# Delta rule of a hybrid block: two heads per sweep, and four heads per sweep with its copies in two portions

## Chip, cores and metric

The kernel runs on one core of one Trainium2 chip. The metric is the device time of one execution in microseconds (us), the median of the executions taken; the profile's span goes from the first to the last instruction of one execution.

## What is computed

One layer of a bidirectional encoder block on 256 tokens of 2048 channels: an input projection whose columns feed an mLSTM branch, a gated delta rule branch with 16 heads of 128, and merge gates, then an output projection and a SwiGLU. All of it is float32. The part that the change touches is the delta rule, forward and backward in time, head by head:

```python
    qkv = jax.nn.silu(centred_depthwise_conv(b_qkv, gdn_conv_w))
    ...
    a_mat = jnp.eye(CHUNK, dtype=jnp.float32) + (
        betac[..., :, None] * jnp.einsum('nbhid,nbhjd->nbhij', kc, kc) * decay_strict)
    t_mat = lax.linalg.triangular_solve(
        a_mat, jnp.broadcast_to(jnp.eye(CHUNK, dtype=jnp.float32), a_mat.shape),
        left_side=True, lower=True, unit_diagonal=True)
    ...
    o_b = bidirectional(gated_delta_chunkwise, (q_b, k_b, v_b), (beta[0], log_decay[0]), (beta[1], log_decay[1]))
    o_b = rms_norm(o_b.transpose(0, 2, 1, 3), gdn_norm_w.reshape(B_HEADS, B_DV)).reshape(bsz, t, B_V)
```

## The kernel before

**Projections.** A weight tile of 1 MB arrives by DMA on SyncE's queue and is used in two halves. Of each half ScalarE makes a high part `wh` (line 181 in `fjob`, 213 in `tjob`), VectorE the rest `wl` (lines 183 and 215), and TensorE multiplies high by high, high by low and low by high. `wh` and `wl` have three buffers each, so ScalarE can make a new `wh` only when TensorE is through with the half three before. `fjob` makes the b jobs (the delta rule's q, k and v: three jobs of two halves per head, 24 matmuls of 128x256 a half) and the a jobs; `tjob` makes everything else (ma and mb for the merge gates, z, v, o), 12 matmuls of 128x512 a half. The jobs that nothing waits for at once are *fills*: `fill(n)` issues n halves of the next one in the list.

**Order.** Every engine works through its own queue in the order in which the program issues. What shall not stand ahead of the next `wh` is appended to a list `behind`; `settle()`, called right after each `wh` copy, issues what is in it. `pump()`, called once per half, issues another piece of the adaptive modulation now and then: one multiplication of a 128x2048 tile on VectorE (line 125, `ada`) with its DMA on SyncE; it is held back in the first three steps of a sweep (`held`).

**A head of the delta rule.** After each of its b jobs comes the convolution (`gdn_conv`: copy into a padded tile `pad`, line 346; ScalarE's first tap `cv`, line 349; four taps on VectorE, line 351; SiLU to `kq` or `vf`, line 354). Then comes the head's first phase (`gdn_phase1`, in two pieces): decays (line 653), `kqh` and `kql` (660, 661), squares `sqkq` (663), on TensorE `vps` (666: vf turned; 668: sums of squares), `nn` and `vv` (678, 688), on TensorE `ks` (699 to 701), on VectorE the masked products `mi`, `mb`, `gg`, `at` (706 to 716), their 32x32 diagonal blocks to memory by GpSimd's queue, and on ScalarE the off-diagonal corners `cc` (738, 741).

**A group of four heads.** `gdn_invert` inverts all 32x32 blocks of a group on VectorE, beside fills. Then `gdn_phase2(g, p)` makes two heads in each of two sweeps, p = 0 and 1, in nine steps with small matmuls (128x32 to 128x128) that each need what ScalarE or VectorE made of the step before: p1 (line 822) and its masked copy `pt` (823); p2 (831), transposed on VectorE and copied into `X` (834 to 838); p3 (844), `pt` (845), copies into `UL` (852); p4 (856) into `UL` (857, 858); pa (868, 869), scaled into `z` (872, 873); pb (880) and `r` (881); pc and its copies; po (890 to 895), with its squares (918) and the scaling by `scaled` (923 and following); px (902) into `obt` (906), stored from ScalarE's queue (907).

Between the steps the loop takes halves from `stream`, which holds the b jobs of the heads of the next group that the sweep prepares, lets each head's first phase follow two and four halves after its last b job, and goes over to fills when the b jobs are used up. How many halves follow each step stands in the tables `after` (first sweep of a group), `second` and, for the last group, `last`:

```python
        for p in range(2):
            pieces = stream(4 * g + 2 * p + 4)
            ...
                for _ in range(last[n] if g == 3 else second[n] if p else after[n]):
                    next(pieces)
```

At the end of a sweep the loop takes halves until the first phases of the sweep's heads are done; after the second it puts the group's z job at the head of the fills and begins the next inversion. In the last group the next heads are none: its sweeps take fills, and begin the mLSTM (`first2`).

## Time and profile before

| what | value |
|---|---|
| time, median of 3 runs | 1948.41 us (1947.84 to 1948.59) |
| time of the profiled execution | 1949.3 us |
| its span | 1947.4 us |
| TensorE busy | 1920.7 us, 99% |
| VectorE busy | 1406.5 us, 72% |
| ScalarE busy | 1032.7 us, 53% |
| mean granted TensorE clock | 0.995 |

The four groups lie between about 310 and 980 us of the span; ahead of them are the first projections, and behind them the mLSTM's rest and the SwiGLU. In the profile PE is TensorE's matmuls, PEld its weight loads, DVE is VectorE, ACT ScalarE, POOL GpSimd and SP SyncE. A busy share is a mean over stages; what an engine waits for stands in the waits. TensorE's clock is granted in windows of about 3.41 us, at full or at half speed.

### The profile page before, as it was taken

The numbers are of one execution on the slowest core, as the hardware profiler recorded it, in microseconds if no ns is written. First come the engines' busy times: TensorE is split into PE (matmuls) and PEld (weight loads), VectorE is DVE, ScalarE is ACT, GpSimd is POOL, SyncE is SP. The second block draws the span as 40 slices with busy tenths as digits, with TensorE's granted clock in tenths as the row PEclk, the third lists the DMA queues.
The fourth block names the chain that finished last, engine by engine and source line by source line (L and its number), as shares of the span: only waits on it lengthen the run. The fifth ranks groups of instructions, "written<-read, shape, count | busy, mean of one in ns | idle before, by whom it ended". The sixth has DMA issues, their size and how long they took to land.

```text
span 1947.4 us, 27209 instructions
## 1 busy us (share of the span) xinstructions
PE 1920.7 (99%) x10436; PEld 1704.7 (88%) x10436; DVE 1406.5 (72%) x2084; ACT 1032.7 (53%) x1564; POOL 124.1 (6%) x223
## 2 busy tenths in 40 slices
PE   8999999999999999999999999999999999999997
PEld 7888889998999899889788888888888888888886
DVE  6788886898788789877577988765665655555554
ACT  3147656765776587565544444644444444444443
POOL 0001220111011101120100000200000000000000
PEclk9999999999999999999999999999999999999999
DMA  9997676666666767686777998577677665565553
GB/s 398 421 358 236 188 257 247 207 230 226 233 213 206 244 216 237 208 296 243 254 290 267 357 348 322 201 248 253 242 251 258 240 218 198 205 206 210 196 208 136
DMA packets 80773, 485.68 MB, mean 249 GB/s; under 512 B 11433, under 2 KB 17137, under 8 KB 26625
## 3 DMA queue, kind: packets, MB, share of 16 engines
q1 hardware_dynamic: 64368, 451.02, 64.2%
q0 software_dynamic: 8672, 17.88, 4.4%
q10 hardware_dynamic: 7602, 15.03, 2.0%
q8 instruction: 82, 1.34, 0.3%
q14 instruction: 49, 0.40, 0.1%
HBM read 467.07 MB, written 16.82 MB: 248 GB/s over the span
## 4 chain that ended last, share of the span: by engine, by line
PE 88%; DVE 4%; DMA 4%; ACT 2%; issue 1%; POOL 0%; SPq 0%; DVEq 0%; POOLq 0%
PE acc_up L249 4%; PE acc_up L248 4%; PE acc_up L247 4%; PE acc_gt L248 4%; PE acc_d L248 4%; PE acc_gt L249 4%; PE acc_d L247 4%; PE acc_d L249 4%; PE acc_gt L247 4%; DMA ra<-ada 3%; PE acc_b L186 3%; PE acc_b L188 3%; PE acc_b L187 3%; PE acc_o L247 2%; PE acc_o L249 2%; PE acc_o L248 2%
## 5 line engine op out<-in xcount | busy, mean ns | idle before, releaser
L215 DVE TENSOR_TENSOR wl_d<-raw_d,wh_d 128x1024 fp32r<-128x1024 f32 x88 | 107.7, 1225 | 105.9 <-ACT wh_d L213 105.9
L215 DVE TENSOR_TENSOR wl_up<-raw_up,wh_up 128x1024 fp32r<-128x1024 f32 x88 | 107.7, 1225 | 100.7 <-ACT wh_up L213 100.7
L215 DVE TENSOR_TENSOR wl_gt<-raw_gt,wh_gt 128x1024 fp32r<-128x1024 f32 x88 | 107.7, 1224 | 76.9 <-ACT wh_gt L213 76.9
L186 PE MATMUL acc_b<-hh,wh_b 128*128 128x256 f32 x576 | 162.7, 283 | 0.0
L213 ACT ACTIVATE wh_d<-raw_d 128x1024 fp32r<-128x1024 f32 x88 | 92.9, 1056 | 126.8 <-PE acc_d L248 118.0
L188 PE MATMUL acc_b<-hh,wl_b 128*128 128x256 f32 x576 | 159.4, 277 | 0.1
L187 PE MATMUL acc_b<-hl,wh_b 128*128 128x256 f32 x576 | 159.1, 276 | 0.0
L213 ACT ACTIVATE wh_gt<-raw_gt 128x1024 fp32r<-128x1024 f32 x88 | 92.9, 1056 | 121.7 <-PE acc_gt L248 75.7
L213 ACT ACTIVATE wh_up<-raw_up 128x1024 fp32r<-128x1024 f32 x88 | 92.8, 1056 | 108.0 <-PE acc_up L248 77.0
L125 DVE SCALAR_TENSOR_TENSOR ada<-ada,crow 128x2048 f32<-128x2048 f32 x64 | 146.2, 2284 | 0.0
L247 PE MATMUL acc_up<-wh_up,hfh 128*128 128x512 f32 x352 | 133.4, 379 | 0.0
L248 PE MATMUL acc_up<-wh_up,hfl 128*128 128x512 f32 x352 | 133.4, 379 | 0.0
L249 PE MATMUL acc_up<-wl_up,hfh 128*128 128x512 f32 x352 | 133.4, 379 | 0.0
L247 PE MATMUL acc_gt<-wh_gt,hfh 128*128 128x512 f32 x344 | 131.6, 383 | 0.0
L248 PE MATMUL acc_gt<-wh_gt,hfl 128*128 128x512 f32 x344 | 130.5, 379 | 0.3 <-DVE hfl L1473 0.3
L248 PE MATMUL acc_d<-wh_d,ffl 128*128 128x512 f32 x344 | 130.5, 379 | 0.0
L249 PE MATMUL acc_gt<-wl_gt,hfh 128*128 128x512 f32 x344 | 130.4, 379 | 0.0
L247 PE MATMUL acc_d<-wh_d,ffh 128*128 128x512 f32 x344 | 130.4, 379 | 0.0
L249 PE MATMUL acc_d<-wl_d,ffh 128*128 128x512 f32 x344 | 130.4, 379 | 0.0
L595 PE MATMUL first<-x,raw 128*128 128x256 f32 x488 | 109.5, 385 | 5.4 <-ACT x L587 5.4
L595 PEld LDWEIGHTS first<-x,raw 128*128 128x128 f32 x488 | 93.0, 192 | 22.0 <-ACT x L587 9.4
L187 PEld LDWEIGHTS acc_b<-hl,wh_b 128*128 128x128 f32 x576 | 111.4, 193 | 0.1
(403 smaller groups left out, 5296.1 us busy)
## 6 DMA issues: line engine op xcount, KB each, us to landing
ada<-ada SPq DMA_DIRECT2D x64, 1024.0 KB, 5.0
raw_gt<-wgu SPq DMA_DIRECT2D x44, 1024.0 KB, 4.9
raw_up<-wgu SPq DMA_DIRECT2D x44, 1024.0 KB, 4.9
raw_d<-wd SPq DMA_DIRECT2D x44, 1024.0 KB, 4.8
raw_b<-winb SPq DMA_DIRECT2D x36, 1024.0 KB, 5.2
ra<-ada SPq DMA_DIRECT2D x30, 1025.0 KB, 14.9
raw_z<-wint SPq DMA_DIRECT2D x16, 1024.0 KB, 4.9
raw_v<-wint SPq DMA_DIRECT2D x16, 1024.0 KB, 5.4
```

Source lines behind the costliest of these rows:

```text
L125: order(V.scalar_tensor_tensor(raw, raw, 1.0, row_c[:, :D], ALU.mult, ALU.mult, accum_out=mod[:, c : c + 1]))
L186: PE.matmul(o, wh[:, k], woven(hh[:, kk]), start=kk == 0, stop=False)
L187: PE.matmul(o, wh[:, k], woven(hl[:, kk]), start=False, stop=False)
L188: PE.matmul(o, wl[:, k], woven(hh[:, kk]), start=False, stop=kk == KB - 1)
L213: order(S.activation(wh, raws[u][:, k0 : k0 + 2], AF.Copy), early)
L215: order(V.tensor_tensor(wl, raws[u][:, k0 : k0 + 2], wh.bitcast(F32), ALU.subtract), early or beside[0])
L247: order(PE.matmul(ps[t], xh[:, kk, c], woven(wh[:, k]), start=kk == 0, stop=False), early and steps > 1)
L248: PE.matmul(ps[t], xl[:, kk, c], woven(wh[:, k]), start=False, stop=False)
L249: PE.matmul(ps[t], xh[:, kk, c], woven(wl[:, k]), start=False, stop=kk == last)
L595: PE.matmul(first[o], raw[:, o], x[:, b], start=b == 0 and o % 2 == 0, stop=b == KB - 1 and o % 2 == 1)
```

## The change

All four heads of a group go through one sweep (`gdn_solve`), so that every step has eight small products in one run (`order` keeps them in the order of the program) where there were twice four. The two PSUM tiles of a step hold two heads each. Most copies of a step are made in two portions: `in_two` issues the first at once and appends the second to `behind`, so that it stands after the next `wh`. A head's first phase follows three and five halves after its last b job. `pt`, `r` and `on` share one buffer, `Et` takes that of `utmp`, and `z` holds four heads. One stream per group holds the b jobs of all four next heads, 24 halves, which fill the new table `after` exactly; a sweep then takes five fill halves where two sweeps took eight, and the three others come later. The first mLSTM heads begin their next step at steps 5 and 7 of the last group.

```diff
-        cg = cgs[g] = bk.tile([P, 2, 4, P], F32, tag="z", bufs=1, name=f"cg{g}").rearrange("p k m c -> p k (m c)")
+        cg = cgs[g] = bk.tile([P, GRP, 4, P], F32, tag="z", bufs=1, name=f"cg{g}")[:, 0:2].rearrange("p k m c -> p k (m c)")
...
-    def gdn_phase2(g, p):
-
-        hd = [heads.pop(4 * g + 2 * p + e) for e in range(2)]
...
+    def in_two(f):
+        f(0)
+        behind.append(lambda: f(1))
+    def gdn_solve(g):
+        hd = [heads.pop(4 * g + h) for h in range(GRP)]
+        th = [(t, h) for t in range(2) for h in range(GRP)]
+        m8 = lambda a: a.rearrange("p (m c) -> p m c", m=8)
+        turned_ = lambda name: bk.tile([P, 8, P], F32, tag="pt", bufs=1, name=f"{name}_{g}")
+        p1 = gps(f"p1_{g}")
+        pt0 = turned_("pt0")
+        for m, (t, h) in enumerate(th):
+            order(PE.matmul(p1[:, m * 32 : (m + 1) * 32], hd[h][0][:, 0, t], R[:, 0, m], start=True, stop=True), m)
+        in_two(lambda i: V.tensor_tensor(
+            pt0[:, 4 * i : 4 * i + 4].rearrange("p m (b c) -> p m b c", b=4),
+            m8(p1[:, 0 : 2 * P])[:, 4 * i : 4 * i + 4].unsqueeze(2).broadcast_to([P, 4, 4, 32]),
             nxt.unsqueeze(1).unsqueeze(3).broadcast_to([P, 4, 4, 32]), ALU.mult,
+        ))
+        yield
+        p2 = gps(f"p2_{g}")
+        for m in range(8):
+            order(PE.matmul(p2[:, m * 32 : (m + 1) * 32], pt0[:, m], R[:, 1, m], start=True, stop=True), m)
+        E_ = p2[:, 0 : 2 * P]
+        Et = bk.tile([P, 2 * P], F32, tag="utmp", bufs=1, name=f"Et{g}")
         V.transpose(Et, E_)
+        S.activation(X[32:64, 1, :, 0], m8(E_[32:64]), AF.Copy)
+        S.activation(X[64:96, 1, :, 1], m8(E_[64:96]), AF.Copy)
+        S.activation(X[32:64, 0, :, 0], m8(Et[0:32]), AF.Copy)
+        S.activation(X[64:96, 0, :, 1], m8(Et[96:128]), AF.Copy)
+        yield
+        p3 = gps(f"p3_{g}")
+        pt1 = turned_("pt1")
+        for m, (t, h) in enumerate(th):
+            order(PE.matmul(p3[:, m * 64 : (m + 1) * 64], hd[h][0][:, 1, t], X[:, 0, m], start=True, stop=True), m)
+        in_two(lambda i: V.tensor_tensor(
+            pt1[:, 4 * i : 4 * i + 4].rearrange("p m (b c) -> p m b c", b=2),
+            m8(p3)[:, 4 * i : 4 * i + 4].unsqueeze(2).broadcast_to([P, 4, 2, 64]),
             half.unsqueeze(1).unsqueeze(3).broadcast_to([P, 4, 2, 64]), ALU.mult,
+        ))
+        def unite(i):
+            for b in (2 * i, 2 * i + 1):
+                c = 32 * (b ^ 1)
+                S.activation(UL[32 * b : 32 * b + 32, b % 2, :, c : c + 32], m8(E_[32 * b : 32 * b + 32]), AF.Copy)
+        in_two(unite)
+        yield
+        p4 = gps(f"p4_{g}")
+        for m in range(8):
+            order(PE.matmul(p4[:, m * 64 : (m + 1) * 64], pt1[:, m], X[:, 1, m], start=True, stop=True), m)
+        S.activation(UL[0:64, 0, :, 64:128], m8(p4[0:64]), AF.Copy)
+        V.tensor_copy(UL[64:128, 1, :, 0:64], m8(p4[64:128]))
+        yield
+        z = bk.tile([P, GRP, 4, P], F32, tag="z", bufs=1, name=f"z{g}")
+        by_bank = lambda name: [gps(f"{name}{i}_{g}").rearrange("p (e k c) -> p e k c", e=2, k=2) for i in range(2)]
         def apply(name, rhs, t0, t1):
+            ps = by_bank(name)
+            for h in range(GRP):
+                o = ps[h // 2][:, h % 2]
+                order(PE.matmul(o[:, 0], UL[:, 0, 4 * t0 + h], rhs(h)[:, 0], start=True, stop=True), h)
+                order(PE.matmul(o[:, 1], UL[:, 1, 4 * t1 + h], rhs(h)[:, 1], start=True, stop=True))
+            def evicted(i):
+                for h in (2 * i, 2 * i + 1):
+                    sg3, o = hd[h][5], ps[h // 2][:, h % 2]
+                    S.activation(z[:, h, t0], o[:, 0], AF.Copy, scale=sg3[:, t0, 0:1])
+                    S.activation(z[:, h, 2 + t1], o[:, 1], AF.Copy, scale=sg3[:, t1, 1:2])
+            in_two(evicted)
+        apply("pa", lambda h: hd[h][3], 0, 1)
+        yield
+        r = turned_("r").rearrange("p (h k) c -> p h k c", h=GRP)
+        pb = by_bank("pb")
+        for h in range(GRP):
             for i in range(2):
+                order(PE.matmul(pb[h // 2][:, h % 2, i], hd[h][1][:, i], z[:, h, 3 * i], start=True, stop=True), h or i)
+        def left(i):
+            for h in (2 * i, 2 * i + 1):
+                V.tensor_tensor(r[:, h], hd[h][3][:, ::-1], pb[h // 2][:, h % 2], ALU.subtract)
+        in_two(left)
+        yield
+        apply("pc", lambda h: r[:, h], 1, 0)
+        yield
+        pos = [gps(f"po{i}_{g}") for i in range(2)]
+        for h in range(GRP):
...
+        on = turned_("on").rearrange("p (h t) c -> p h t c", h=GRP)
+        gdn_norm(g, on, pos, [hd[h][4][:, 2:4] for h in range(GRP)])
         yield
         settle(only="scaled")
+        settle(only="scaled")
+        px = [gps(f"px{i}_{g}") for i in range(2)]
+        for h in range(GRP):
             for t in range(2):
+                c = (2 * (h % 2) + t) * P
+                order(PE.transpose(px[h // 2][:, c : c + P], on[:, h, t], ident), h or t)
+        def away(i):
+            for h in (2 * i, 2 * i + 1):
+                obt = obp.tile([P, T], F32, tag="obt", bufs=2, name=f"obt{4 * g + h}")
+                b = PK_GNW + 4 * g + h
+                S.activation(obt, px[h // 2][:, h % 2 * T : (h % 2 + 1) * T], AF.Copy, scale=pk[:, b : b + 1])
+                S.dma_start(ob_d[g][h], obt)
+        in_two(away)
+        yield
+    def gdn_norm(g, on, pos, rqs):
+        so = bk.tile([P, 3, GRP, 2], F32, tag="so", bufs=2, name=f"so{g}")
+        po = lambda h, t: pos[h // 2][:, (2 * (h % 2) + t) * P : (2 * (h % 2) + t + 1) * P]
+        for h in range(GRP):
+            V.tensor_tensor(so[:, 1, h], rqs[h], rqs[h], ALU.mult)
         sz = szs[g]
+        def squares(i):
+            for h in (2 * i, 2 * i + 1):
+                for t in range(2):
+                    S.activation(on[:, h, t], po(h, t), AF.Square, accum_out=so[:, 0, h, t : t + 1])
+            if i:
+                V.tensor_tensor(so[:, 1], so[:, 1], so[:, 0], ALU.mult)
+                behind.append(part(0))
+        def part(i):
+            def scaled():
+                if not i:
+                    order(S.activation(so[:, 1], so[:, 1], AF.Sqrt, bias=epsc, scale=1.0 / (DK_B * DK_B)))
+                    V.reciprocal(so[:, 1], so[:, 1])
+                    for h in range(GRP):
+                        V.scalar_tensor_tensor(so[:, 2, h], rqs[h], DK_B**-0.5, so[:, 1, h], ALU.mult, ALU.mult)
+                for h in (2 * i, 2 * i + 1):
+                    for t in range(2):
+                        V.scalar_tensor_tensor(
+                            on[:, h, t], po(h, t), so[:, 2, h, t : t + 1], sz[:, t, h * P : (h + 1) * P], ALU.mult, ALU.mult
+                        )
+                if not i:
+                    behind.append(part(1))
+            return scaled
+        in_two(squares)
...
-        for h in range(h0, min(h0 + 2, NH_B)):
+        for h in range(h0, min(h0 + GRP, NH_B)):
...
-            todo += [[2, h], [4, h]]
+            todo += [[3, h], [5, h]]
...
-    after = (0, 1, 2, 1, 2, 2, 2, 2, 4, 0)
-    last = (0, 1, 2, 1, 2, 2, 1, 1, 3, 0)
-    second = (0, 2, 2, 1, 2, 2, 2, 2, 3, 0)
+    after = (0, 2, 3, 3, 3, 3, 3, 3, 4, 0)
+    last = (0, 2, 3, 2, 3, 4, 3, 3, 6, 0)
...
-        pairs = [gdn_phase2(g, p) for p in range(2)]
+        solve = gdn_solve(g)
...
-        for p in range(2):
-            pieces = stream(4 * g + 2 * p + 4)
-            for n in range(1, 10):
-                held[0] = n < 4
-                if p == 0:
-                    next(blocks, None)
-                next(pairs[p], None)
-                if g == 3 and n == (8, 4)[p]:
-                    next(first2[p])
-                for _ in range(last[n] if g == 3 else second[n] if p else after[n]):
-                    next(pieces)
-            for _ in pairs[p]:
-                pass
-            if g < 3:
-                while 4 * g + 2 * p + 5 not in heads:
-                    next(pieces)
+        pieces = stream(4 * g + 4)
+        for n in range(1, 10):
+            held[0] = n < 4
+            next(blocks, None)
+            next(solve, None)
+            if g == 3 and n in (5, 7):
+                next(first2[n // 7])
+            for _ in range((last if g == 3 else after)[n]):
+                next(pieces)
+        for _ in solve:
+            pass
+        if g == 3:
+            settle()
+        else:
+            while 4 * g + 7 not in heads:
+                next(pieces)
```

(`settle(only="scaled")` is called twice ahead of px, since the scaling too is in two portions. What stands in the lines left out of `gdn_solve` are the six matmuls of po for each head, as before.)

**Where the instructions go: ScalarE, end of group 0's sweep.** `b7` is the last head that group 0's sweep prepares, `pad3` to `vf7` its v convolution, `obt0` to `obt3` the outputs of group 0, `ev_ma0` the evacuation of a merge-gate job. Before, the queue reads there:

```order
L213 ACTIVATE wh_mb1_2_0_3820<-raw_mb1_2_3818 128x1024
L346 ACTIVATE pad3_148<-acc_b7_2_3649 128x256
L349 ACTIVATE cv7_2_3726<-pad3_148,pk_77 128x256
L213 ACTIVATE wh_mb1_2_2_3838<-raw_mb1_2_3818 128x1024
L354 ACTIVATE vf7_3506<-cv7_2_3726 128x256
L918 ACTIVATE on0_1_0_3765,so0_1_3767<-po_0_1_3751 128x128 x2
L918 ACTIVATE on0_1_1_3766,so0_1_3767<-po_0_1_3751 128x128 x2
L923 ACT_TABLE_LOAD
```

After the change, behind `wh_mb1_0_0`, a table load, `kq7` and six copies of `cc0`:

```order
L346 ACTIVATE pad3_148<-acc_b7_2_3534 128x256
L926 ACTIVATE obt0_3658<-px0_0_3648,pk_77 128x256
L349 ACTIVATE cv7_2_3642<-pad3_148,pk_77 128x256
L927 DMA ob_d0_122<-obt0_3658 128x256
L926 ACTIVATE obt1_3661<-px0_0_3648,pk_77 128x256
L660 ACTIVATE kqh7_3737<-kq7_3382 128x512
L927 DMA ob_d0_122<-obt1_3661 128x256
L368 ACT_TABLE_LOAD
L368 ACTIVATE ev_ma0_3708<-acc_ma0_0_2341 128x512
L354 ACT_TABLE_LOAD
L354 ACTIVATE vf7_3383<-cv7_2_3642 128x256
L926 ACTIVATE obt2_3670<-px1_0_3649,pk_77 128x256
```

Two outputs, `kqh7` and the `ma` evacuation with two table loads have moved in between `pad3` and `vf7`.

**ScalarE, copies of pa (group 1).** `z1` is the tile that the copies of pa fill, `wh_b` the weights' high parts. Before, for the first two heads:

```order
L349 ACTIVATE cv8_2_4752<-pad2_146,pk_77 128x256
L872 ACTIVATE z1_0_4758<-pa_1_0_4760,sm4_2885 128x128
L873 ACTIVATE z1_0_4758<-pa_1_0_4760,sm4_2885 128x128
L872 ACTIVATE z1_0_4758<-pa_1_0_4760,sm5_3136 128x128
L873 ACTIVATE z1_0_4758<-pa_1_0_4760,sm5_3136 128x128
L181 ACTIVATE wh_b9_1_0_4867<-raw_b9_1_4865 128x1024
```

After the change, for all four:

```order
L181 ACTIVATE wh_b10_0_8_4977<-raw_b10_0_4945 128x1024
L880 ACTIVATE z1_4884<-pa0_1_4885,sm4_2913 128x128
L881 ACTIVATE z1_4884<-pa0_1_4885,sm4_2913 128x128
L880 ACTIVATE z1_4884<-pa0_1_4885,sm5_3220 128x128
L881 ACTIVATE z1_4884<-pa0_1_4885,sm5_3220 128x128
L880 ACTIVATE z1_4884<-pa1_1_4886,sm6_3566 128x128
L881 ACTIVATE z1_4884<-pa1_1_4886,sm6_3566 128x128
L354 ACTIVATE kq9_4698<-cv9_1_4804 128x256
L880 ACTIVATE z1_4884<-pa1_1_4886,sm7_3785 128x128
L881 ACTIVATE z1_4884<-pa1_1_4886,sm7_3785 128x128
```

Here the eight copies stand in one run, a `kq` among them, with no `wh` between the two portions.

**VectorE, first head of the next group (head 8, in group 1's sweep).** `cv8_2` are the taps of its v convolution, `wl_b9` the weights of the next head. Before:

```order
L661 TENSOR_TENSOR kql8_4845<-kq8_4586,kqh8_4844 128x512
L351 SCALAR_TENSOR_TENSOR cv8_2_4752<-pad2_146,pk_77,cv8_2_4752 128x256 x4
L183 TENSOR_TENSOR wl_b9_1_0_4868<-raw_b9_1_4865,wh_b9_1_0_4867 128x1024
L125 SCALAR_TENSOR_TENSOR ada2_7_4749,mod_93<-ada2_7_4749,crow_76 128x2048
L183 TENSOR_TENSOR wl_b9_1_8_4897<-raw_b9_1_4865,wh_b9_1_8_4896 128x1024
L881 TENSOR_TENSOR r1_0_4759<-vv4_2892,pb_1_0_4857 128x256
```

After the change:

```order
L661 TENSOR_TENSOR kql8_4761<-kq8_4456,kqh8_4760 128x512
L183 TENSOR_TENSOR wl_b9_1_0_4726<-raw_b9_1_4723,wh_b9_1_0_4725 128x1024
L351 SCALAR_TENSOR_TENSOR cv8_2_4632<-pad2_146,pk_77,cv8_2_4632 128x256
L125 SCALAR_TENSOR_TENSOR ada2_6_4426,mod_93<-ada2_6_4426,crow_76 128x2048
L351 SCALAR_TENSOR_TENSOR cv8_2_4632<-pad2_146,pk_77,cv8_2_4632 128x256
L183 TENSOR_TENSOR wl_b9_1_8_4774<-raw_b9_1_4723,wh_b9_1_8_4773 128x1024
L351 SCALAR_TENSOR_TENSOR cv8_2_4632<-pad2_146,pk_77,cv8_2_4632 128x256
L183 TENSOR_TENSOR wl_b9_2_0_4814<-raw_b9_2_4811,wh_b9_2_0_4813 128x1024
L351 SCALAR_TENSOR_TENSOR cv8_2_4632<-pad2_146,pk_77,cv8_2_4632 128x256
```

The four taps stood together ahead of the ada row and two `wl`; now the ada row and two `wl` stand between them.

106 lines of the change are left out of this document (9 added, 97 removed).

## The prediction

> **What bounds the kernel now.** I read the first page of the profile, then TensorE's waits, then the windows around the delta rule, then ScalarE's and VectorE's groups there.
>
> ```profile
> span 1947.4 us, 27209 instructions
> PE 1920.7 (99%) x10436; PEld 1704.7 (88%) x10436; DVE 1406.5 (72%) x2084; ACT 1032.7 (53%) x1564; POOL 124.1 (6%) x223
> ```
>
> TensorE is busy for 99% of the span. The change issues the same matmuls, so the time can move only by what TensorE waits, and by the clock it is granted. The waits (total, times, longest, in us):
>
> ```profile
> PE first L595 <- ACT x L587: 5.4, 10, 2.6
> ...
> PE acc_z L249 <- DVE wl_z L215: 2.5, 3, 1.0
> ...
> PE p L831 <- DVE pt L823: 1.2, 1, 1.2
> ...
> PE vps L666 <- ACT vf L354: 0.8, 1, 0.8
> PE pb L880 <- DVE r L881: 0.6, 3, 0.2
> PE acc_a L188 <- DVE wl_a L183: 0.4, 1, 0.4
> PE vps L668 <- ACT sqkq L663: 0.3, 1, 0.3
> ```
>
> The first row is the program's start, which the change doesn't touch. The rows at L831, L880 and L666 are the delta rule's: 1.2 + 0.6 + 0.8 = 2.6 us in all. There is one hidden price besides. In the windows the columns are length, then busy time (instructions) of PE, PEld, DVE, ACT and POOL, then PE's clock, DMA share and GB/s:
>
> ```profile
> 315.00:432.70 117.70, 116.18 (x905) 111.93 (x905) 99.53 (x197) 87.51 (x177) 10.60 (x21) 0.99 0.65 215
> 373.90:377.30 3.40, 2.31 (x19) 2.20 (x20) 3.40 (x6) 1.56 (x6) 2.30 (x5) 1.00 0.32 93
> 377.30:380.72 3.42, 3.42 (x19) 3.42 (x18) 3.00 (x6) 3.11 (x9) 1.27 (x2) 0.50 0.76 235
> 380.72:384.13 3.41, 3.41 (x32) 3.41 (x32) 1.24 (x2) 1.25 (x3) 0.00 (x0) 1.00 0.96 216
> ```
>
> ```profile
> 374.94 1.08 PE L831 MATMUL p<-R,pt 128*128 128x32 f32 x8 [1.18 <-DVE pt L823]
> ```
>
> The 1.18 us wait at L831 falls into the second window, and eight small matmuls follow it; the window after it runs at clock 0.50 and completes 19 matmuls, where the next one, in as long, completes 32. So a wait of about a microsecond beside small matmuls cost 1.2 us and then (32 - 19) / 32 x 3.41 = **1.4 us** more. In the first row, one group's sweep before the change, VectorE is busy for 99.53 of 117.70 us and ScalarE for 87.51: neither bounds the mean, but a burst of work on either can.
>
> **What the change moves.** The heads' matmuls come in groups of eight in place of twice four. Three rows price that:
>
> ```profile
> 315.84 0.36 PE L186 MATMUL acc_b<-hh,wh_b 128*128 128x256 f32 x1
> ...
> 318.60 0.98 PE L831 MATMUL p<-R,pt 128*128 128x32 f32 x8
> 319.41 0.36 PE L186 MATMUL acc_b<-hh,wh_b 128*128 128x256 f32 x1
> ```
>
> Half a b job lasts 318.60 - 315.84 = 2.76 us, a group of four small products (eight instructions) 319.41 - 318.60 = 0.81 us, with no gap at either border. A group of eight is then 1.62 us, twice a group of four: merging saves TensorE nothing, and costs it nothing. A half of a t job is 12 matmuls of 0.216 us, 2.6 us, by the steps of the chain rows:
>
> ```profile
> 424.93 0.22 PE vps L666 x2
> 425.15 0.79 PE vps L668 x8
> ...
> 431.23 0.22 PE ks L699
> ...
> 432.52 0.44 PE px L902 x4
> ```
>
> The rows that price ScalarE's and VectorE's queues (the number behind the bar is busy time, then mean ns of one):
>
> ```profile
> L181 ACT ACTIVATE wh_b<-raw_b 128x1024 fp32r<-128x1024 f32 x23 | 24.2, 1055 | 12.6 <-PE acc_b L187 8.0 <-PE acc_ma L248 2.5 <-PE acc_a L187 1.9
> L349 ACT ACTIVATE cv<-pad,pk 128x256 f32<-128x256 f32 x12 | 6.0, 503 | 0.2
> L354 ACT ACT_TABLE_LOAD x4 | 5.1, 1283 | 0.1
> L346 ACT ACTIVATE pad<-acc_b 128x256 f32<-128x256 f32 x12 | 4.5, 375 | 0.9 <-PE acc_b L188 0.8
> L354 ACT ACTIVATE kq<-cv 128x256 f32<-128x256 f32 x8 | 3.3, 414 | 2.8 <-DVE cv L351 2.7
> L660 ACT ACTIVATE kqh<-kq 128x512 fp32r<-128x512 f32 x4 | 2.5, 630 | 0.1
> L663 ACT ACTIVATE sqkq<-kq 128x512 f32<-128x512 f32 x4 | 2.5, 625 | 0.0
> L738 ACT ACTIVATE cc<-mb 32x64 f32<-32x64 f32 x8 | 2.0, 254 | 0.8 <-DVE mb L707 0.7
> L906 ACT ACTIVATE obt<-px,pk 128x256 f32<-128x256 f32 x4 | 1.7, 472 | 1.8 <-PE px L902 1.8
> L354 ACT ACTIVATE vf<-cv 128x256 f32<-128x256 f32 x4 | 1.7, 419 | 4.7 <-DVE cv L351 4.5
> L741 ACT ACTIVATE cc<-mb 64x128 f32<-64x128 f32 x4 | 1.2, 307 | 0.0
> ```
>
> ```profile
> L183 DVE TENSOR_TENSOR wl_b<-raw_b,wh_b 128x1024 fp32r<-128x1024 f32 x24 | 29.1, 1217 | 5.2 <-ACT wh_b L181 5.1
> L351 DVE SCALAR_TENSOR_TENSOR cv<-pad,pk,cv 128x256 f32<-128x256 f32 x48 | 22.9, 478 | 1.2 <-ACT cv L349 0.8
> L125 DVE SCALAR_TENSOR_TENSOR ada<-ada,crow 128x2048 f32<-128x2048 f32 x6 | 13.7, 2284 | 0.0
> ```
>
> ```profile
> L368 ACT ACTIVATE ev_ma<-acc_ma 128x512 f32<-128x512 f32 x2 | 1.1, 593 | 0.0
> ```
>
> *Removed.* The second sweep of a group goes, and with it the p2 wait in it (1.2) and the half-clock window behind it (1.4). r in two portions, with three halves of b matmuls at every step, should end the pb waits (0.6). The first phases a piece later end the one wait of vps for vf (0.8). Sum: **-4.0 us**. In two portions, the copies of a step no longer hold up the weights' next high part, which is on ScalarE ahead of its matmuls; that already waits 12.6 us for TensorE over 23 instructions (its row), so I cost this gain at nothing. One sweep takes 5 fill halves in place of 8; the other three run later in a stretch with nothing but fills, at the same 2.6 us each: nothing.
>
> *Added, first head of the next group.* In groups 0 to 2 vps of that head now stands after three b halves and the group of eight at p4: from the end of its v matmuls TensorE has 3 x 2.76 + 1.62 = 9.9 us. On the other side lie, one behind the other, pad (0.375), wh (1.055), on VectorE three wl (1.217), four cv (0.478) and an ada row (2.284) = 7.8, about 0.1 of hand-over, and vf (0.42): 9.8 us. That is a tie. ScalarE's rows ahead (a kq, a kqh of 0.63, four copies of UL) can come later than assumed by up to 2.6 us (1.055 + 0.63 + two of 0.414, and the hand-over), so the wait lies between 0 and 2.6 us. I take 0.6, near the 0.8 of the same wait before: 3 x 0.6 = **+1.8**.
>
> *Added, the end of group 0's sweep.* Here the last head of the next group, the outputs of this group and a merge-gate job (ma) meet on ScalarE. From the end of the last b half the queue holds, ahead of vf: wh of the mb job (1.055; its buffer comes free only then), a table load (1.283), kq (0.414), six corner copies (4 x 0.254 + 2 x 0.307 = 1.6), pad (0.375), obt (0.472), cv (0.503), obt (0.472), kqh (0.63), a table load, ev_ma (0.593), a table load again, and vf (0.419): 10.4 us. Neighbours overlap by up to 0.1 us each and two stores are issued among them, so 9.2 to 11.1. TensorE reaches vps after px (0.88) and three t halves (7.8): 8.7 us. The wait is 0.5 to 2.4; I take 0.9. Then sqkq stands behind two obt, a table load, ev_ma and itself (3.4), while TensorE has vps and the six ks (0.22 + 6 x 0.22 = 1.5): 1.6 more, the overlaps taken off. Behind it wh and wl of the next mb half (1.055 + 1.217) against vps' 0.79 and two matmuls (1.2): 0.9. Together **+3.4**. Waits of that size in the company of small matmuls made the half-clock window above, so **+1.4**.
>
> *Added, the other ends.* In group 1 sqkq of the last head stands behind one more obt: 0 to 1.7 us, taken 0.7, between the 0.3 of the same wait before and the upper end. In group 2 the squares go ahead of the second obt pair: 0 to 1.0, taken 0. *Moved away:* one acc_z wait (1.0) stands right behind group 0's sweep; TensorE, held up ahead of it, arrives there after wl_z is ready: **-1.0**.
>
> *Queues besides.* The output stores are issued from ScalarE's queue as before, 16 of them; the ada row that each sweep sheds is multiplied later, under dense fills. VectorE may be late by 0 to 0.9 us per group for the wl behind r (two subtractions now stand together); TensorE's queue there has b matmuls of earlier halves in front, so I take 0, and keep 0.9 for the range.
>
> **A rule weighed against a row.** The Trainium skill, "TensorE: Matmul & The Clock Gate", section "Why this matters for your kernels", asks for no idle gaps above about 3 us between bursts, since one idle window halves the clock. The trace differs: the 1.18 us wait sufficed. By the page the end of group 0 would cost no slow window and the sum would be 1.4 us less. Another row of the trace has slow clock with no wait at all; it stands behind 24 matmuls of 128x1:
>
> ```profile
> 943.90:947.40 3.50, 3.50 (x32) 3.40 (x31) 0.28 (x3) 2.09 (x7) 2.08 (x4) 0.99 0.68 213
> 947.40:950.80 3.40, 3.40 (x5) 1.32 (x5) 0.45 (x4) 1.77 (x3) 0.47 (x1) 0.50 0.96 316
> ```
>
> So what counts seems to be how much of the array works in a window, and a group with small matmuls and a wait is the bad case. I go by the rows.
>
> **Sum.** -4.0 + 1.8 + 3.4 + 1.4 + 0.7 - 1.0 = **+2.3 us**. The profiled execution took 1949.3 us (span 1947.4, and 1.9 around it), 0.9 above the median of the three runs, 1948.41. I put the difference on the median: 1948.4 + 2.3 = **1950.7 us**.
>
> **Rivals.**
> *Faster: ScalarE has run ahead.* If ScalarE still holds the lead that its 12.6 us of waiting for TensorE suggest, all added waits are hidden, and both gains stay: -4.0 - 1.0 = -5.0, **1943.4 us**. For it: in a sweep ScalarE is idle for 30 of 117.7 us. Against it: at the ends of the sweeps its queue can't start earlier than the end of the last b half, because wh waits there for its buffer.
> *Slower: ScalarE's queue is the bound at the ends of all three sweeps.* It decides when the queue from the last b half to vf takes longer than TensorE's 8.7 us. With plain sums and no overlap the waits are 5.3 at the end of group 0 (2.4 + 1.9 + 1.0), 1.7 for group 1 and 1.0 for group 2, each with its half-clock window, 3 x 1.4 = 4.2; with the first heads' 1.8, less 4.0 and 1.0: +9.0, **1957.4 us**. For it: three table loads of 1.28 us stand in group 0's queue, and one wait already brought a slow window. Against it: groups 1 and 2 have no ma job in the middle of the queue.
> *The change doesn't do what it says.* In the new order the two portions of the pa copies stand with no weights' copy between them; if the same holds in time elsewhere and the waits of before stay as they are, the time is that of before, **1948.4 us**.
>
> **Chances.** The forecast's case gets 0.45, the faster rival 0.22, the slower 0.28, the last 0.05. A measurement of this kernel tells about 0.2% from no change, 3.9 us: "same" runs from 1944.5 to 1952.3. The forecast's own range is 1947 (its first-head waits and the lower ends at group 0) to 1955 (one group with the 2.6 us, and the upper end at group 0); of its 0.45, 0.33 lie within "same" and 0.12 above. So faster 0.22, same 0.33 + 0.05 = 0.38, slower 0.28 + 0.12 = 0.40. The range goes from the faster rival's 1943 to the slower one's upper side, 1958, which holds each single bound (all three first-head waits at 2.6: +6.0, 1956.7).
>
> **What would show it.** Right: no wait at p2 nor at pb; waits of TensorE for vf of the first head in groups 0 to 2, for vf and then sqkq at the end of group 0, with a row of windows at clock 0.50 behind it. Wrong: no wait of over 0.5 us at the end of group 0 (then the ScalarE sum is too high, and the time is below 1948), slow windows at the ends of groups 1 and 2, or waits of the b matmuls for wl all through the sweeps, which would say that VectorE, 85% busy there, is the bound that I put at nothing.

## The result, and the profile after

| | before | after |
|---|---|---|
| time, median | 1948.5 us | 1983.87 us |
| ratio | | 1.018 (95% interval 1.017 to 1.019) |
| span of the profiled execution | 1947.4 us | 1979.5 us |
| TensorE's waits from 300 to 1100 us of the span | 5.0 us | 26.5 us |
| windows at half clock in that stretch | 3 | 9 |

The change makes the kernel 35 us slower, 1.8%; the forecast was 1950.7, with 1958 as the upper end of its range. The first lines of the page:

```profile
span 1979.5 us, 27143 instructions
## 1 busy us (share of the span) xinstructions
PE 1931.2 (98%) x10436; PEld 1708.7 (86%) x10436; DVE 1399.8 (71%) x2068; ACT 1024.3 (52%) x1523; POOL 124.1 (6%) x223
```

TensorE has the same 10436 instructions, and VectorE and ScalarE have fewer than before and are no busier. So no engine got more work: what grew is TensorE's waiting, and the time that it spends at half clock. The stretch with the delta rule, 300 to 1100 us (columns as in the windows of the prediction), first before, then after:

```profile
300.00:1100.00 800.00, 794.97 (x5131) 726.17 (x5130) 642.27 (x1146) 501.03 (x891) 80.30 (x149) 0.99 0.71 242
```

```profile
300.00:1100.00 800.00, 773.55 (x4979) 703.81 (x4979) 604.46 (x1096) 477.17 (x833) 80.32 (x149) 0.98 0.67 227
```

Not busy: 800 - 794.97 = 5.0 us before, 26.5 after, so 21.4 us of new waits. In the same stretch the clock goes to half 9 times in place of 3, and a window of 3.41 us at half clock loses half of itself, 1.7 us: 6 x 1.7 = 10.2. Together 31.6 of the 32.1 us by which the span grew. TensorE's waits after the change:

```profile
PE vps L666 <- ACT vf L354: 13.2, 6, 2.8
PE acc_z L249 <- DVE wl_z L215: 7.2, 3, 4.1
PE first L595 <- ACT x L587: 6.1, 11, 3.1
PE vps L668 <- ACT sqkq L663: 2.4, 2, 1.6
...
PE acc_b L188 <- DVE wl_b L183: 2.3, 3, 0.8
```

The waits at p2 and pb are gone, as the change wants it. In their place stand six waits of `vps` for `vf`: 13.2 us where there were 0.8. They are the first and the last head of each of three groups. **The first head**, on TensorE, ScalarE and VectorE (start, duration, instruction, idle time before it; in the changed kernel p4 is line 863, an output line 926 and its store line 927):

```profile
341.73 1.90 PE L863 MATMUL p<-X,pt 128*128 128x64 f32 x16
...
348.14 0.44 PE L666 MATMUL vps<-cst,vf 128*128 128x128 f32 x2 [1.78 <-ACT vf L354]
```

```profile
336.63 1.67 ACT L807 ACTIVATE UL<-cg 32x256 f32<-32x256 f32 x4
338.32 0.63 ACT L660 ACTIVATE kqh<-kq 128x512 fp32r<-128x512 f32 x1
338.98 0.39 ACT L346 ACTIVATE pad<-acc_b 128x256 f32<-128x256 f32 x1
...
347.67 0.42 ACT L354 ACTIVATE vf<-cv 128x256 f32<-128x256 f32 x1 [3.02 <-DVE cv L351]
```

```profile
341.88 2.29 DVE L125 SCALAR_TENSOR_TENSOR ada<-ada,crow 128x2048 f32<-128x2048 f32 x1
...
344.49 1.22 DVE L183 TENSOR_TENSOR wl_b<-raw_b,wh_b 128x1024 fp32r<-128x1024 f32 x1
...
346.02 1.22 DVE L183 TENSOR_TENSOR wl_b<-raw_b,wh_b 128x1024 fp32r<-128x1024 f32 x1
```

TensorE arrives at 346.4 and waits 1.78 us. Three halves and p4 earlier, at 346.4 - 9.9 = 336.5, the head's v product was ready, but ScalarE took it over (`pad`) only at 338.98, behind four copies of `UL` and `kqh`. Then the taps shared VectorE with the ada row and the weights' low parts, and ScalarE itself waited 3.02 us for the last tap. The same wait, 1.78 us each time, stands in groups 1 and 2.

**The last head**, here of group 1's sweep, on ScalarE and on TensorE:

```profile
596.91 0.47 ACT L926 ACTIVATE obt<-px,pk 128x256 f32<-128x256 f32 x1
...
597.41 0.33 ACTq L927 DMA_DIRECT2D ob_d<-obt  x1
597.79 0.47 ACT L926 ACTIVATE obt<-px,pk 128x256 f32<-128x256 f32 x1
...
603.06 0.47 ACT L926 ACTIVATE obt<-px,pk 128x256 f32<-128x256 f32 x1 [3.13 <-DMA ob_d<-obt]
603.44 0.41 ACT L354 ACTIVATE vf<-cv 128x256 f32<-128x256 f32 x1
```

```profile
603.89 0.69 PE L666 MATMUL vps<-cst,vf 128*128 128x128 f32 x2 [2.81 <-ACT vf L354]
606.22 1.87 PE L668 MATMUL vps<-ones,sqkq 128*128 128x1 f32 x8 [1.63 <-ACT sqkq L663]
```

Four outputs now leave in one go through two `obt` buffers. The third must wait until the first one's store, issued at 597.41, has landed; ScalarE stands still for 3.13 us, and `vf`, whose taps have long been made, stands behind it in the queue. TensorE waits 2.81 us for `vf` and 1.63 us for `sqkq`. The clock in these windows:

```profile
600.00:603.40 3.40, 1.09 (x10) 0.90 (x9) 1.95 (x5) 0.34 (x1) 0.00 (x0) 1.00 0.99 322
603.40:606.80 3.40, 1.27 (x5) 0.88 (x5) 0.00 (x0) 2.07 (x6) 0.52 (x1) 0.50 0.36 100
606.80:610.20 3.40, 3.40 (x12) 2.97 (x12) 2.79 (x3) 3.37 (x5) 0.00 (x0) 0.50 0.27 87
610.20:613.70 3.50, 3.50 (x17) 3.39 (x16) 3.06 (x5) 1.16 (x3) 0.00 (x0) 0.51 0.80 262
```

One disturbed place costs three windows at half clock. From 606.8 to 610.2 TensorE is never idle, but several of its products are still the 128x1 of `vps`, and the next window is slow again; behind 610.2 to 613.7, whose last three microseconds hold 128x256 products alone, the clock is back.

**The z waits** behind the sweeps grew too, on GpSimd, VectorE and TensorE:

```profile
807.68 0.51 POOL L729 DMA_DIRECT2D uu<-inst_d  x1 [6.12 <-DMA ada<-ada]
```

```profile
810.84 0.19 DVE L767 TENSOR_TENSOR utmp<-uu 64x30 f32<-64x30 f32 x1 [5.73 <-DMA uu<-inst_d]
```

```profile
815.42 0.79 PE L249 MATMUL acc_z<-wl_z,hh 128*128 128x512 f32 x1 [4.09 <-DVE wl_z L215]
```

The last head's blocks go to memory and back before the inversion can begin. VectorE has the inversion's first operations in its queue ahead of a `wl_z`, so their late data hold up the weights: 2.44 us behind group 0 and 4.09 behind group 2, where it was about 1 us before. How late they are depends on the way through memory: from the transposition of the blocks (line 716) to the landing of `uu` it takes 10.7 us behind group 0 and 12.0 behind group 2. The four small stores of a head, which landed 1.7 to 1.9 us after their issue before, take 1.7 to 5.0 and 1.7 to 6.1 us here; in group 2 a 1 MB tile of z weights and an ada row, issued at 800.23 and 800.61, are on their way beside them.

### The profile page after: what moved, and what is told of

Its sections match the earlier page's. It is cut to its first block, busy times and chain, and to the rows that moved or that the text cites. A ratio compares the mean times of both kernels' runs of the same rounds, so it can differ in the third digit from the quotient of the medians.

```text
span 1979.5 us, 27143 instructions
## 1 busy us (share of the span) xinstructions
PE 1931.2 (98%) x10436; PEld 1708.7 (86%) x10436; DVE 1399.8 (71%) x2068; ACT 1024.3 (52%) x1523; POOL 124.1 (6%) x223
## 4 chain that ended last, share of the span: by engine, by line
PE 76%; DVE 8%; DMA 7%; ACT 5%; issue 2%; POOL 0%; SPq 0%; ACTq 0%; DVEq 0%; POOLq 0%
PE acc_up L249 4%; PE acc_up L247 4%; PE acc_up L248 4%; PE acc_gt L248 4%; PE acc_d L248 4%; PE acc_gt L249 4%; PE acc_d L247 4%; PE acc_d L249 4%; PE acc_gt L247 4%; DMA ra<-ada 3%; PE acc_b L186 2%; PE acc_o L247 2%; PE acc_b L188 2%; PE acc_o L248 2%; PE first L595 2%
## 5 line engine op out<-in xcount | busy, mean ns | idle before, releaser
L188 PEld LDWEIGHTS acc_b<-hh,wl_b 128*128 128x128 f32 x576 | 110.3, 192 | 3.4 <-DVE wl_b L183 3.4
```

Source lines behind the costliest of these rows:

```text
L188: PE.matmul(o, wl[:, k], woven(hh[:, kk]), start=False, stop=kk == KB - 1)
```

## The experiments

Theory A: the waits for `vf`, made by the outputs' stores and by VectorE's chain, and the half-speed windows behind them. Rival B: VectorE is simply too densely loaded. Rival C: the later first phases are to blame. The times are medians, each with its ratio to the kernel before, run on the same chip.

### The outputs in the dead z tile

```diff
-                obt = obp.tile([P, T], F32, tag="obt", bufs=2, name=f"obt{4 * g + h}")
+                obt = z[:, h, 0:2].rearrange("p k c -> p (k c)")
```

> The changed kernel, with the four outputs obt written into the z tile, which nothing reads any more by then, in place of two obt buffers; nothing else differs. Theory A (at the ends of the sweeps the third obt waits on ScalarE until the first one's store has landed, and vf and sqkq stand behind it; the waits there then bring half-speed windows): ScalarE's 5.4 us of waits for ob_d go, TensorE's wait for vf at the end of group 1 falls from 2.8 to about 0.5 and of group 2 from 2.2 to about 1.4, sqkq's 1.6 goes, and of the five half-speed windows there at least three go (1.5 us each): 10 to 13 us faster than the change, about 1972. Group 0's end stays as it is. Theory B (VectorE is too densely loaded in a sweep without fills, the outputs are beside the point): under 3 us.

Measured: 1986.09 us (ratio 1.019, 1.017 to 1.021), no gain. Its waits:

```profile
PE vps L666 <- ACT vf L354: 12.3, 6, 4.8
PE acc_z L249 <- DVE wl_z L215: 7.8, 3, 4.7
...
PE ks L699 <- ACT kqh L660: 2.9, 2, 1.7
```

ScalarE's waits for the stores at the output copies are gone and the wait at the end of group 1 fell from 2.81 to 0.38 us, as theory A has it. With the buffers free, though, the program gets another order: three outputs now stand ahead of the merge-gate copy and of `vf` at the end of group 0, `kqh` behind them, and the wait there is 4.8 us. The z waits stayed, and the clock was at half for 13 windows in place of 9. By its size theory A failed: taking away one wait of a queue that is late anyway only moved the wait.

### The ada row one step later

```diff
-            held[0] = n < 4
+            held[0] = n < 5
```

> The changed kernel, with the ada row held back for one step more of each sweep (n < 5 in place of n < 4), so that it is no longer between the taps of the first head's v. Theory A: TensorE's three waits of 1.8 us for vf of the first heads go, little else: 4 to 6 us faster than the change, about 1978.5. Theory B (VectorE's load decides all over the sweep): the row comes later and waits move with it, so less than 2 us.

Measured: 1969.8 us (1.011, 1.009 to 1.013), 14 us faster than the change: more than theory A's 4 to 6, and far more than B's 2.

```profile
PE vps L666 <- ACT vf L354: 9.0, 5, 3.9
PE vps L668 <- ACT sqkq L663: 3.4, 2, 1.9
...
PE acc_z L249 <- DVE wl_z L215: 0.7, 1, 0.7
```

The first heads wait no more. In two groups the second head waits instead (1.4 us), since the row now stands between its taps, and the end of group 1 waits 3.89. That the wait goes where the row goes shows the row's part; the rest of the gain is elsewhere, above all at the z waits, which fell from 7.2 to 0.7 us. Holding the row back moves its DMA too: in group 2 no ada row is issued beside the block stores any more, they land within 1.7 to 2.7 us, and the blocks' way through memory takes 7.8 us behind group 0 and 8.5 behind group 2.

### First phases later still

```diff
-            todo += [[3, h], [5, h]]
+            todo += [[4, h], [6, h]]
```

> The changed kernel, with each head's first phase four and six halves after its last b job in place of three and five. Theory A: every wait for vf has 2.6 to 2.8 us more cover: the first heads' (3 x 1.8) and the last heads' (2.8, 2.8, 2.2) go, and the half-speed windows with them: 15 to 25 us faster than the change, 1960 to 1969; the inversion's data come a half later, so the z waits (2.4 and 4.1) may grow by up to 2.6 each. Theory B: within 3 us, since the work is the same.

Measured: 1952.04 us (1.0025, 1.0014 to 1.0036), 32 us faster than the change, more than expected. No `vps` waits for `vf` any more. What is left are waits for `sqkq` behind the outputs' stores, and a z wait:

```profile
PE vps L668 <- ACT sqkq L663: 4.4, 3, 3.0
...
PE acc_o L247 <- ACT wh_o L213: 2.4, 1, 2.4
PE acc_z L249 <- DVE wl_z L215: 1.8, 2, 1.1
```

```profile
413.68 0.48 ACT L926 ACTIVATE obt<-px,pk 128x256 f32<-128x256 f32 x1 [3.77 <-DMA ob_d<-obt]
```

One line of the source decides nearly all of the 35 us. The z waits did not grow, though the phases come later, so it is not the later phase that makes them. In the kernels with one sweep the z wait behind group 2 goes with the blocks' way through memory: it takes 12.0 to 12.8 us in the four kernels with a wait of 4.0 to 4.8 us (the change, outputs in z, copies at once, first head later), 9.9 to 10.5 in the five with 0.5 to 1.1, and 8.5 and 9.2 in the two with none (ada row later; phases 5 and 7 with the outputs in z). (With the phases at two and four halves the z wait lies ahead of the inversion and does not belong here.) The stalled last head alone does not make it: with the ada row later, group 0's last head still stalls TensorE for 1.65 and 1.90 us, and no z wait follows.

### The later first phases in the kernel before

```diff
-            todo += [[2, h], [4, h]]
+            todo += [[3, h], [5, h]]
```

> The kernel before, with one part of the change alone: first phases three and five halves after the last b job in place of two and four. Theory A (the later phases are not the cause): within 3 us of before, the wait of 0.8 for vf gone and the z waits longer by up to 2 us. Rival C (the later first phase is the cause: it pushes the last head into the outputs and the inversion): over 10 us slower than before.

Measured: 1965.62 us (1.009, 1.008 to 1.011): 18 us slower than before, so rival C's number is right here and theory A's is not. But C's reason, the outputs and the inversion, is not what the waits show:

```profile
PE pb L880 <- DVE r L881: 6.1, 5, 1.7
...
PE acc_z L249 <- DVE wl_z L215: 3.7, 3, 2.6
PE px L902 <- DVE on L929: 3.6, 1, 3.6
```

Three of the five waits for `r` are at the first head of a sweep. Its `vps`, which stood ahead of `pb` before (340.99 and 342.01 us), now stands behind it (345.70), so TensorE asks for `pb` 1.2 us sooner (340.79); and VectorE has taps of the `cv`, `wl_b` copies and an ada row ahead of `r`. The longest wait, 3.6 us at px, lies in the last group, whose sweeps prepare no heads; what made it was not traced. Three and five halves is a bad place in both kernels, with different waits.

### Later phases and the outputs in z

```diff
-            todo += [[3, h], [5, h]]
+            todo += [[4, h], [6, h]]
...
-                obt = obp.tile([P, T], F32, tag="obt", bufs=2, name=f"obt{4 * g + h}")
+                obt = z[:, h, 0:2].rearrange("p k c -> p (k c)")
```

> The changed kernel with first phases four and six halves after the last b job, and the outputs written into the z tile in place of two obt buffers. Theory A' (what costs is how long TensorE's cover is between the end of a head's v product and its vps, each wait priced with the half-speed windows that follow it): with the cover given, ScalarE's waits for the stores at the ends are the next in line; the sqkq waits (3.0 and 1.2) and one wait for wh_o (2.4) that the later phases left go, and some of the four half-speed windows behind them: 5 to 12 us faster than with the later phases alone, 1940 to 1947. Theory D (the outputs' buffers are of no account, as in the kernel with the early phases): within 2 us of 1952.

Measured: 1943.09 us (0.9973, 0.9961 to 0.9985): 9 us better than with the later phases alone, and 0.3% faster than before. The `sqkq` waits and the five half-clock windows behind the sweeps of groups 0 to 2 are gone; the one in the last group is left:

```profile
300.00:1100.00 800.00, 796.42 (x5163) 729.96 (x5162) 639.92 (x1134) 492.58 (x851) 80.25 (x149) 1.00 0.71 245
```

3.6 us of waiting, less than before the change. The same edit that gave nothing with early phases gives 9 us once the heads are covered.

### The same, with the ada row one step later

```diff
-            held[0] = n < 4
+            held[0] = n < 5
```

> As the last one, with the ada row held back for one step more. Theory A': the first heads have 0.8 us to spare with the later phases, so the ada row between their taps costs TensorE nothing any more: within 3 us of the last one. Theory B (VectorE's load is what bounds a sweep): 5 us or more faster, as it was by 14 us with the early phases.

Measured: 1948.1 us (1.0007, 0.9997 to 1.0016), 5 us slower than the last, a little beyond theory A's 3 us and the opposite of B. The waits from 300 to 1100 us are the same (3.5 us); a new one of 2.6 us stands much later, behind 1200 us. The first kernel with this edit has it too (2.4 us), and so has the kernel with the phases at two and four halves (1.2 us), which lacks the edit, so the edit alone does not make it. Just ahead of it a wait for `wl_o` grew from 0.4 to 1.7 us, and two windows at half clock begin there, at 1231 us. Together that is 1.3 + 2.6 + 3.4, less the one window of the last kernel, 1.7: 5.6 us, against 4.8 between the two spans. Why `xn` comes late was not traced:

```profile
PE pxn L1386 <- ACT xn L1377: 2.6, 1, 2.6
```

### Both portions at once

```diff
         f(0)
-        behind.append(lambda: f(1))
+        f(1)
```

> The changed kernel with one part undone: both portions of every copy are issued at once, ahead of the next high part. Theory A': the portions are neither cause nor cure, the cover at vps stays as short: within 6 us of the change, 1978 to 1990, with the waits for vf within 1 us of the change's. Rival E (the second portion, put behind the next high part, comes too late and that makes the waits): over 10 us faster than the change.

Measured: 1981.79 us (1.017, 1.015 to 1.019), within the 6 us.

```profile
PE vps L666 <- ACT vf L354: 8.6, 3, 4.6
```

By the time, the portions are neither cause nor cure. But the waits for `vf` did not stay within 1 us of the change's, as theory A' had it: the first heads wait 0.2 us at most, the ends of groups 0 and 1 4.6 and 3.8. What one place gained the others lost.

### First phases as early as before

```diff
-            todo += [[3, h], [5, h]]
+            todo += [[2, h], [4, h]]
```

> The changed kernel with one part undone: first phases two and four halves after the last b job, as before. Theory A': every vps has one b half (2.8 us) less of cover, so the first heads' wait grows from 1.8 to about 4.5, the last heads' from 2.2 to 2.8 to about 5, the middle heads keep about 1 us: 16 us or more of waiting and some half-speed windows on top, 2000 to 2015. Rival C (the later first phases are what made the change slow, as they made the kernel before slower by 18 us): back to within 10 us of before.

Measured: 1985.21 us (1.019, 1.018 to 1.021), about the change's time and far from the 2000 or more that I expected, but no return to before either.

```profile
PE vps L666 <- ACT vf L354: 10.1, 10, 1.4
...
PE acc_b L188 <- DVE wl_b L183: 2.8, 3, 0.9
PE acc_a L188 <- DVE wl_a L183: 2.7, 3, 1.3
```

Ten heads wait now, none longer than 1.4 us, and the waits for low parts grew. So cover can't be subtracted head by head: that part of theory A was wrong. A likely reason, not tested, is that each stall gives the other engines time.

### One head later alone

For the last head of each group (and, in the second kernel, with `h % GRP == 0`, for the first):

```diff
-            todo += [[3, h], [5, h]]
+            late = h % GRP == GRP - 1
+            todo += [[3 + late, h], [5 + late, h]]
```

> The changed kernel with the first phase of the last head of each group alone one half later (four and six), the other heads as in the change. Theory A': the ends of the sweeps hold most of the cost; their vf waits (2.8, 2.8, 2.2) and most of the half-speed windows there go, as they did with all phases later, the sqkq waits come instead (up to 4), the first heads' 3 x 1.8 and the wl waits of 2.3 stay: 15 to 22 us faster than the change, 1962 to 1969. Rival F (the first heads, which start the chain of lateness, hold most of it): under 8 us faster.

> The changed kernel with the first phase of the first head of each group alone one half later. Theory A': the three waits of 1.8 us go, the ends of the sweeps stay as they are: 5 to 8 us faster than the change, 1976 to 1979. Rival F (the ends are late because the first heads are): over 15 us faster.

Measured: the last head alone 1967.49 us (1.0115, 1.010 to 1.013), the first alone 1975.61 us (1.0155, 1.014 to 1.017): 16 and 8 us faster than the change, both about as expected. Their sum is 25 of the 32 us that all heads bring, so about half of the gain is at the ends of the sweeps, a quarter at the first heads, and the rest comes with the other heads or with all together. The last-head kernel keeps the first heads' three waits of 1.8 us:

```profile
347.54 0.44 PE L666 MATMUL vps<-cst,vf 128*128 128x128 f32 x2 [1.79 <-ACT vf L354]
```

### One half later again, and both portions at once with the good placement

Both start from the kernel with later phases and outputs in z; the one has `[[5, h], [7, h]]`, the other `f(1)` at once.

> First phases five and seven halves after the last b job, outputs in the z tile. Theory A': with four and six no vps waits for vf any more, so more cover buys nothing; the last head's data for the inversion come one half later and the z waits may grow by up to 2 us: 1942 to 1947. If cover were still short somewhere, it would be faster than 1940.

> First phases four and six halves after the last b job, outputs in the z tile, and both portions of every copy at once. Theory A': the portions matter little here too: within 4 us of the same kernel with portions (1943). Rival G (once the phases are covered, it is the high part behind the copies that is late, so the portions are what makes the one sweep pay): over 5 us slower than that, with waits of the b matmuls for wh or wl.

Measured: five and seven halves 1954.07 us (1.0044, 1.0029 to 1.0058), outside what I expected; the portions at once 1942.19 us (0.9983, 0.9972 to 0.9994), within 1 us of the kernel with portions. In the first one the cover is ample, and the waits are at other places:

```profile
PE acc_b L188 <- DVE wl_b L183: 5.1, 6, 2.7
PE acc_yb L249 <- DVE wl_yb L215: 4.4, 1, 4.4
```

So of the places tried the phase has one good one in this sweep; half a b job to either side costs 11 us or more.

**All profiles in one sum.** The waits are 800 us less TensorE's busy time from 300 to 1100 us, the windows those at half clock in that stretch:

| kernel | span, us | waits, us | windows | span - waits - 1.7 x windows |
|---|---|---|---|---|
| before | 1947.4 | 5.0 | 3 | 1937.3 |
| the change | 1979.5 | 26.5 | 9 | 1937.7 |
| outputs in z | 1987.0 | 27.8 | 13 | 1937.1 |
| phases 4, 6 | 1956.8 | 10.5 | 6 | 1936.1 |
| phases 4, 6, outputs in z | 1940.8 | 3.6 | 1 | 1935.5 |
| copies at once | 1981.5 | 26.3 | 12 | 1934.8 |
| last head later | 1962.4 | 18.3 | 4 | 1937.3 |
| phases 4, 6, in z, at once | 1938.9 | 4.3 | 0 | 1934.6 |
| first head later | 1974.6 | 24.4 | 9 | 1934.9 |
| phases 5, 7, outputs in z | 1954.5 | 12.6 | 3 | 1936.8 |
| before, phases 3, 5 | 1962.4 | 16.2 | 6 | 1936.0 |
| ada row later | 1968.7 | 13.8 | 9 | 1939.6 |
| phases 4, 6, in z, ada row later | 1945.6 | 3.5 | 0 | 1942.1 |
| phases 2, 4 | 1981.0 | 24.0 | 7 | 1945.1 |

The spans lie 48 us apart. In eleven profiles the last column agrees within 3.1 us. The three at the end are those with the `pxn` wait (2.4, 2.6 and 1.2 us) and two half-clock windows (3.4 us) behind 1100 us; with these taken off they come to 1933.8, 1936.1 and 1940.5. So waits and half-clock windows are nearly the whole of the differences.

## Why the prediction was wrong

The signs of its parts were mostly right, and its slower rival (ScalarE's queue at the ends of the sweeps, with half-clock windows) named the place; the sizes were far off, and so was its 1957. Two of its own signs of being wrong appeared: slow windows at the ends of groups 1 and 2, and waits for `wl_b`.

The step that failed is the comparison, head by head, of the time that TensorE gives a head (its cover: 9.9 us for the first heads, 8.7 at group 0's end) with the chain to `vf`, and the net zero for half-clock windows. The sum put 0.6 us at each first head, 0.9 at group 0's end and nothing on `vf` at the ends of groups 1 and 2; the runs show six waits of 1.8 to 2.8 us, 13.2 in all, and one more half of cover takes them all away and 32 of the 35 us with them. Of the span's 32.1 us the sum had 2.3. The rest is 10.2 from windows, 6.0 from the ends of groups 1 and 2, 5.7 from the z waits, 3.5 from the first heads, 2.3 from `wl_b`, and about 2 in small pieces.

- **Removed, -4.0.** Right: p2's and pb's waits and the window behind p2 are gone, and the old `vf` wait. But the b half behind pb now waits for `wl_b`, three times 0.8 us, near the upper bound of 0.9 that I had put beside a zero.
- **First heads, +1.8.** The mechanism was right, the size wrong: 3 x 1.78 = 5.3. The tie of 9.8 against 9.9 took `pad` at the moment the product ended; it came 2.5 us later. I had bounded that by 2.6 and then chosen 0.6 by the row of another place. The kernel with the first head later brought 8 us.
- **End of group 0, +3.4 and one window.** The waits are 2.80 (vf), 0.78 (sqkq) and 0.13 (wl): 3.7 in all. That the sum of 3.4 came so near is luck: `vf` was taken at 0.9, with 2.4 as its upper end, `sqkq` at 1.6 and `wl` at 0.9. Two windows at half clock, not one.
- **The other ends, +0.7.** Here a term was put at nothing that should have had a price. The prediction read "the output stores are issued from ScalarE's queue as before" and priced them at nothing. Before, a sweep had two outputs and two buffers; with four, the third waits for a landing. The waits are 2.81 + 1.63 us in group 1 and 2.21 in group 2, with five half-clock windows. The number of buffers stood in the code, and the durations in the list of DMA issues; I counted the stores' issue and not their landing. That explains group 1: with the outputs in z its wait for `vf` is 0.38 us. It explains little of group 2, where 1.80 of the 2.21 stay, and curing it alone brought no time, so the landing is not the whole of this term.
- **z, -1.0.** Wrong in sign: +4.7. I let TensorE arrive later and left the chain behind it where it was, but the last head's blocks feed the inversion, and that stands ahead of `wl_z` on VectorE. Their way through memory, which took 10.7 and 12.0 us, stands in no term of the sum.
- **Half-clock windows, net 0.** Measured six more, 10.2 us, a third of the loss. The price for one was about right (1.4 against 1.7), their number was not: I counted one for each place at most, and there are two or three at the end of every sweep; in the one traced above, a window without any idle time but with small products was followed by another slow one.

On the rule of the Trainium skill weighed there ("TensorE: Matmul & The Clock Gate", "Why this matters for your kernels": no gaps above about 3 us): the rows decide against it again, since from 300 us on only one wait in the changed kernel, 4.09 us at z, is longer than 3 us, and nine windows went to half clock.

What stays open: why the same kernel but for two buffers has 13 windows in place of 9 can be told row by row, but not foretold; and of the ada row's 14 us it was not separated how much comes from its place between the taps and how much from the z waits, which fell when its transfer moved.

## What to carry to other kernels

When work of two rounds is put into one, count the buffers of everything that leaves at its end: a third store through two buffers makes the queue behind it wait for a landing. Compare for every product the time that the matrix engine gives it with the time that its chain needs, from the moment its engine really takes it up, and move the consumer rather than thin out the chain. A fix that gives nothing alone may be worth much behind another: the outputs' place gave nothing with short cover and 9 us with enough.

## What the runs showed of the hardware

The clock's windows take no account of the program: in every profile here the changes of the clock lie whole multiples of 3.413 us apart. In the first kernel with outputs in z, the wait of the first head is 1.8 us in every group; behind it the clock stays full in group 0 and is half in group 1, although PE is busy for 1.63 and 1.61 of the 3.40 us around it:

```profile
346.60:350.00 3.40, 1.63 (x15) 1.44 (x15) 3.30 (x7) 1.75 (x3) 0.00 (x0) 1.00 1.00 405
...
536.00:539.40 3.40, 1.61 (x15) 1.44 (x14) 3.30 (x6) 1.89 (x3) 0.00 (x0) 0.99 0.97 340
539.40:542.80 3.40, 3.40 (x19) 3.40 (x18) 3.29 (x11) 3.33 (x6) 0.00 (x0) 0.50 0.86 282
```

The windows follow each other every 3.413 us, so 56 of them before the 539.4 of the third row a border lies at 348.3: it cuts the first stretch and its wait in two, while the second stretch is one window from end to end. So a wait of this size costs 1.8 us or 3.5, by where it falls, and a shift of a microsecond far ahead can change that. A border inside the wait does not always help: with the last head alone later, the wait of group 1's first head, 530.28 to 532.06, is cut at 530.86, and the clock is half behind 534.27 all the same. A store of 128 KB, 3.1 us from issue to landing in the median of the changed kernel, took 6.2 us in the mean of the two at the end of group 1, where the DMA engines were 99% busy (the window from 600 us). The Trainium skill, "DMA: Bandwidth & Descriptors", section "Latency and other measured facts", has memory latency go up to 2 us under load; the direction agrees; the 3.1 us more here are those of a whole store, not of one access.
